# Fixed tile rotation two units deep, quartered low parts of w_down's sums, and a last layernorm with one GpSimd pass

## The chip, the cores and the metric

The kernel runs on one core of one Trainium2 chip. The metric is the device time of one execution in microseconds (us), the median over several runs. Five engines work side by side, each in its own order: TensorE (PE, matrix products into the PSUM banks; PEld is its weight load), VectorE (DVE), ScalarE (ACT), GpSimd (POOL) and SyncE (SP), which issues all DMAs here.

## What is computed

One decoder layer in float32 for 1024 tokens of width 1024: a token mixer (one input projection, a spatial gating half and a causal convolution half, one output projection) with a residual layernorm, then a gated MLP with a second one. The MLP and the last layernorm are what most of the change touches:

```
h    = causal_depthwise_conv(x1 @ w_up, conv_f_w, conv_f_b)      # 1024 x 5632, conv width 3
gate, val = h[:, :2816], h[:, 2816:]
ffn  = (silu(gate) * val) @ w_down                               # 2816 x 1024
out  = layernorm(1.189 * x1 + ffn, ln2_g, ln2_b)                 # rows of 1024
```

## The kernel before

Every float32 operand of a matrix product is split in two: a high part, rounded to the type that TensorE multiplies (a CAST on ACT), and a low part, what is left over (a subtraction on POOL or DVE). A product is three matmuls: high by high, high by low, low by high. The helper `split` does it for all of them, so the casts stand at L75 and the subtractions at L78.

**Input and output projections.** Sixteen column blocks of w_in are loaded through the pool `raw` (6 tiles of 128x1024), several ahead of use, then eight row blocks of w_out through the same pool (`load_wo`). `ln1` writes x1; `x1_T` and `x1_T2` transpose it.

**Up projection.** w_up's columns are cut into NF = 22 units: unit f is 128 gate and 128 value columns by all 1024 tokens. Unit 0 is a plain product (`first_steps`, 96 matmuls of 128x512: 2 column groups, 2 token halves, 8 row blocks, 3 matmuls each); its own matmuls alternate with the transposes of the second half of x1 (`x1_T2`), and `x1_sums` makes four sums of x1's quarters, t1 to t4, and splits them. From unit 1 on a unit is one step of Winograd's form of Strassen's product (`unit`): 7 products of 12 matmuls, 84 instead of 96. They take x1's quarters (b11, b21, b22 and t1 to t4) and the unit's weights and four sums of them. `prep_unit(f)` makes these: sums s1, s2 (tile `sa`) and s3, s4 (tile `sb`) on DVE, and seven splits (`wa`, `wb`, four `ws`, `wd`). When a unit's products are in PSUM, `conv3` applies the width-3 convolution: one ACT pass and two DVE passes of 128x1023 for the gate (`cg`), then as many for the value (`cv`), a SiLU, the product of the two, and a store to `hd[f]` in DRAM. Gate and value sums take two PSUM tiles a unit, and there are tiles for two units: a unit's first product writes where the unit before the last one was, so it waits until that one's `cg` passes have read it.

**Down projection.** It is of the same form: w_down's blocks are taken in NP = 11 pairs of units (kp), and each needs sums of w_down's quarters. Those are made during the up projection, at times that the table `sum_at` sets (a unit for each kp): `sum_load` reads two blocks of 512 KB (`dq`), `sum_prep` makes four sums on DVE (L813 to L816), two casts of 128x1024 on ACT (`dsh`) and two subtractions of 128x1024 on POOL, and stores the four results of 512 KB to DRAM. In the down loop `down_prep` is called ahead of a block: `wop_prep` reads them back (`ds`), loads and splits the plain parts (`db` to `dh`, `dl`), `hop_prep` does as much for the activations (`hr` to `ho`, sums `hs`). PE's products of this phase are at L930, and DVE adds each result to the row tiles x1r (L941, L946). At the end `finish` normalizes two row blocks, p and p+4, of a token pair, and `finish_last` those of the last pair.

**What sets the order.** Each engine executes in its own order, fixed when the program is built by a scheduler. It places the instructions by a simulated timeline: program order, `tc.high_priority` and `tc.issue_after` move them. Tiles come from pools of a few buffers each; a tile that is asked for waits until the last reader of the oldest one is done, so which buffer is reused, and when, comes out of the schedule.

## Time and profile before

| | us |
|---|---|
| median of 3 runs (lowest to highest) | 1046.07 (1046.02 to 1049.15) |
| the profiled execution | 1044.81 |
| its span in the trace | 1043.0 |
| PE busy in the span | 961.4 (92%) |
| DVE busy | 787.2 (75%) |
| POOL busy | 622.3 (60%) |
| ACT busy | 460.7 (44%) |

The times of the trace count from the start of the span; 1.8 us of the profiled execution lie outside it. The mean clock that TensorE was granted over the span is 0.963 of full. The stretches are: input and output projections to 301 us, up projection from 301.13 to 780.6 us (unit 0 to 336.16), down projection from 782 to 1017 us, the last row blocks to 1043 us. Of the chain that ended last, PE holds 57% and DVE 23%. A row of the timeline view gives start, duration, engine, line, operation, output and inputs, shape, and in brackets how long the engine had been idle and what ended that. Matmuls overlap: the pitch is read from their starts.

### The profile page before, as it was taken

How to read it: one execution, taken by the hardware profiler on the slowest of the kernel's cores; microseconds unless marked ns; L12 is line 12 of the kernel's file. 1: busy time of each engine (PE TensorE's matmuls, PEld its weight loads, DVE VectorE, ACT ScalarE, POOL GpSimd, SP SyncE). 2: the span in 40 equal slices, each digit the busy share in tenths (PEclk: the TensorE clock that was granted, in tenths of full speed). 3: DMA queues.
4: the chain of work that ended last, by engine and by line, in shares of the span. 5: the costliest groups of instructions: out<-in, count | busy, mean ns of one | idle time of the engine just before them, and what ended most of it. 6: DMA issues, size and time to landing. Idle time of an engine off the chain costs nothing.

```text
span 1043.0 us, 11987 instructions
## 1 busy us (share of the span) xinstructions
PE 961.4 (92%) x4200; PEld 781.5 (75%) x4200; DVE 787.2 (75%) x1062; ACT 460.7 (44%) x673; POOL 622.3 (60%) x391
## 2 busy tenths in 40 slices
...
GB/s 350 80 41 62 61 81 61 57 26 75 188 52 30 122 101 236 187 142 122 236 167 142 101 202 174 186 104 162 170 325 341 199 195 195 214 177 185 47 28 134
DMA packets 51627, 150.11 MB, mean 144 GB/s; under 512 B 5104, under 2 KB 16752, under 8 KB 51568
## 3 DMA queue, kind: packets, MB, share of 16 engines
...
q14 instruction: 26, 0.21, 0.1%
...
## 4 chain that ended last, share of the span: by engine, by line
PE 57%; DVE 23%; POOL 6%; issue 5%; DMA 5%; ACT 3%; SPq 0%; POOLq 0%; DVEq 0%; ACTq 0%
PE ps L215 15%; PE xy L930 12%; PE upv L624 10%; PE po L537 8%; PE upg L624 8%; DVE cg L636 3%; POOL dq L78 3%; DMA hr<-hd 3%; PE z L930 2%; DVE sa L693 2%; POOL ws L78 2%; DVE sa L694 2%; DVE cv L636 2%; DVE sb L699 1%; DMA ur<-in_w_up 1%
## 5 line engine op out<-in xcount | busy, mean ns | idle before, releaser
L930 PE MATMUL xy<-ds,ho 128*128 128x512 f32 x528 | 132.5, 399 | 11.1 <-DVE x1r L946 6.2
L263 DVE SCALAR_TENSOR_TENSOR acc<-ybin,cv,acc 128x512 f32<-128x512 f32 x196 | 134.3, 744 | 0.9 <-ACT acc L257 0.3
L946 DVE TENSOR_TENSOR x1r<-xy,x1r 128x512 f32<-128x512 f32 x117 | 80.3, 690 | 65.3 <-PE xy L930 64.9
L930 PEld LDWEIGHTS xy<-ds,ho 128*128 128x128 f32 x528 | 99.7, 191 | 38.1 <-DVE x1r L946 10.0
L78 POOL TENSOR_TENSOR ws<-sb,ws 128x512 fp32r<-128x512 f32 x42 | 58.0, 1380 | 62.9 <-ACT ws L75 62.9
L78 POOL TENSOR_TENSOR ho<-hr,ho 128x1024 fp32r<-128x1024 f32 (+1 forms) x24 | 55.6, 2315 | 50.3 <-ACT ho L75 50.3
L78 POOL TENSOR_TENSOR ws<-sa,ws 128x512 fp32r<-128x512 f32 x42 | 60.2, 1435 | 33.2 <-ACT ws L75 26.8
L624 PE MATMUL upv<-b11h,wa 128*128 128x512 f32 x168 | 57.0, 400 | 21.3 <-DVE cg L636 21.2
L930 PE MATMUL xy<-dh,ho 128*128 128x512 f32 x220 | 64.3, 396 | 6.2 <-POOL dh L78 3.7
L78 POOL TENSOR_TENSOR dq<-dq,dsh 128x1024 fp32r<-128x1024 f32 x22 | 57.3, 2619 | 10.0 <-ACT dsh L75 7.8
L624 PE MATMUL upv<-t2h,ws 128*128 128x512 f32 x168 | 57.4, 403 | 6.0 <-ACT pa L713 5.9
L624 PE MATMUL upg<-t1h,ws 128*128 128x512 f32 x168 | 61.7, 430 | 0.4 <-DVE upg L715 0.4
L636 DVE SCALAR_TENSOR_TENSOR cg<-upg,cv,cg 128x1023 f32<-128x1023 f32 (+4 forms) x46 | 56.6, 1230 | 6.1 <-ACT cg L633 5.2
L624 PE MATMUL upg<-b21h,wb 128*128 128x512 f32 x168 | 58.0, 390 | 0.0
L75 ACT CAST ho<-hr 128x1024 fp32r<-128x1024 f32 (+1 forms) x24 | 23.5, 978 | 77.2 <-issue 48.8
L636 DVE SCALAR_TENSOR_TENSOR cv<-upv,cv,cv 128x1023 f32<-128x1023 f32 (+4 forms) x46 | 56.6, 1230 | 1.2 <-ACT cv L633 0.5
L78 POOL TENSOR_TENSOR wa<-ur,wa 128x512 fp32r<-128x512 f32 x21 | 29.0, 1381 | 46.2 <-ACT wa L75 46.2
L624 PEld LDWEIGHTS upv<-b11h,wa 128*128 128x128 f32 x168 | 32.1, 191 | 32.2 <-issue 25.3
L693 DVE TENSOR_TENSOR sa<-ur 128x512 f32<-128x512 f32 x21 | 32.8, 1560 | 30.6 <-POOL ws L78 22.9
L624 PE MATMUL upv<-t3h,ws 128*128 128x512 f32 x168 | 55.1, 389 | 0.0
L624 PE MATMUL upv<-t4h,wd 128*128 128x512 f32 x168 | 55.1, 389 | 0.0
L624 PE MATMUL upg<-b22h,ws 128*128 128x512 f32 x168 | 55.1, 389 | 0.0
...
## 6 DMA issues: line engine op xcount, KB each, us to landing
ur<-in_w_up SPq DMA_DIRECT2D x44, 512.0 KB, 3.5
hd<-cg SPq DMA_DIRECT2D x22, 512.0 KB, 4.2
dq<-in_w_down SPq DMA_DIRECT2D x22, 512.0 KB, 6.0
dsh<-dsh SPq DMA_DIRECT2D x22, 512.0 KB, 2.7
dsl<-dq SPq DMA_DIRECT2D x22, 512.0 KB, 2.7
ds<-dsh SPq DMA_DIRECT2D x22, 512.0 KB, 4.4
ds<-dsl SPq DMA_DIRECT2D x22, 512.0 KB, 5.2
...
```

The costliest lines, as they stand in the source:

```text
L75: nc.scalar.copy(hi, raw)
L78: lo_eng.tensor_tensor(out=lo, in0=raw, in1=hi.bitcast(F32), op=ALU.subtract)
L215: nc.tensor.matmul(ps[hf] if isinstance(ps, list) else ps[:, ts(hf, 512)], wt[:, ts(k, P)], xt(k, hf), start=first and k == 0, stop=(not f ...
L263: nc.vector.scalar_tensor_tensor(out=xs(0) if k == 0 else acc, in0=xs(k), scalar=w(k), in1=first if n == 0 else acc, op0=ALU.mult, op1=ALU ...
L537: nc.tensor.matmul(po[:, ts(hf, 512)], a, b[:, ts(hf, 512)], start=first and i == 0, stop=last and i == 2)
L624: nc.tensor.matmul(out, w[a][:, ts(k, P)], x[b][k // 2][:, k % 2], start=first and k == 0 and i == 0, stop=last and k == 3 and i == 2, ski ...
L636: nc.vector.scalar_tensor_tensor(out=c[:, o:b], in0=ps[:, o - sh : b - sh], scalar=w(k), in1=c[:, o:b], op0=ALU.mult, op1=ALU.add,)
L693: tt(out=s1, in0=a21, in1=a22, op=ALU.add)
L694: tt(out=s2, in0=s1, in1=a11, op=ALU.subtract)
L699: tt(out=s4, in0=a12, in1=s2, op=ALU.subtract)
L930: nc.tensor.matmul(bank, hops[n][q][a][:, i, ts(j, P)], wops[kp][q][b], start=first and i == 0 and c == 0, stop=last and i == len(ks) - 1 ...
L946: nc.vector.tensor_tensor(out=dst if out is None else out, in0=bank, in1=dst, op=ALU.add)
```

## The change

It has six parts.

1. **Staging tiles.** The pool `raw` of 6 becomes two groups of 3 in the same memory, `raw` and `raw2`; loads of w_in and w_out have only the first.
2. **Start of the up projection.** `x1_sums` makes t1 and t2 only; `x1_sums2` makes t3, t4 and all splits after the last of those. Unit 0's second token half is computed in quarters of 256 columns, so that the first of them needs only two of the four transposed row blocks. Unit 1 becomes a plain product as well (96 matmuls instead of 84).
3. **Fixed rotation.** `keep` makes a tile once and returns it again: w_up's blocks, sa, sb, pa in two copies each (unit f uses copy f mod 2), operand tiles `wop` in eight, down weights `W` in three sets, `ho` and `hr` in two.
4. **Sums of w_down.** The table `sum_at` takes kp in every second unit, and the sums are cut in quarters of 128x512 (`sum_part`), called between the splits of `prep_unit`: a cast, a subtraction and two stores of 256 KB each. For kp = 0 they are made last, stay in SBUF (`dz`) and are split in `wop_prep`: nothing is stored or read back for it.
5. **Down operands.** The order of the loads at the end of the up projection is other, and `hop_load(1)` follows the loads of x1.
6. **Last layernorm.** In `finish` the row block p is treated like p+4: one DVE pass, an ACT pass and one POOL addition, the last two in halves, in place of an ACT pass and two POOL passes.

```diff
-    ) as ap_, tc.tile_pool(name="b", bufs=16) as bp, tc.tile_pool(name="raw", bufs=6) as rawp, tc.tile_pool(
+    ) as ap_, tc.tile_pool(name="b", bufs=16) as bp, tc.tile_pool(name="raw", bufs=3) as rawp, tc.tile_pool(
...
+
+        def raw2(name, shape=(P, 1024), dt=F32):
+            return rawp.tile(list(shape), dt, tag="raw2", name=name, bufs=3)
...
+        kept = {}
+
+        def keep(name, make):
+            if name not in kept:
+                kept[name] = make()
+            return kept[name]
...
-                    t = xt(f"ur{f}_{i}")
+                    t = keep(("ur", f % 2, i), lambda: xt(f"ur{f % 2}_{i}"))
...
         def op_tile(name, n):
-            if n % 2:
-                t = wp.tile([P, 1024], F32R, tag=("whi", "wlo")[n // 2 % 2], name=name, bufs=2)
...
-                t = A(F32R, name)
+            def make():
+                if n % 2:
+                    return wp.tile([P, 1024], F32R, tag=("whi", "wlo")[n // 2 % 2], name=f"wop{n % 8}", bufs=2)
+                return A(F32R, f"wop{n % 8}")
+
+            t = keep(("o", n % 8), make)
             return t[:, 0:512], t[:, 512:1024]
...
-        nop = [0]
+        nop = [1]
...
-            sa, sb = xt(f"sa{f}"), xt(f"sb{f}")
+            sa, sb = (keep((q, f % 2), lambda: xt(f"{q}{f % 2}")) for q in ("sa", "sb"))
...
+            part(0)
             tt(out=s3, in0=a11, in1=a21, op=ALU.subtract)
             w[7] = split_op(s3, f"ws3{f}")
+            part(1)
             tt(out=s4, in0=a12, in1=s2, op=ALU.subtract)
             w[3] = split_op(s4, f"ws4{f}")
+            part(2)
             w[4] = split_op(a22, f"wd{f}")
+            part(3)
...
+        def first_steps(f, q, hf, ks, part=None):
+            a0, a1 = (0, 512) if part is None else (part * 256, part * 256 + 256)
+            for k in ks:
+                for n, (a, b) in enumerate(((0, 0), (0, 1), (1, 0))):
+                    nc.tensor.matmul(
+                        ups[f][q][:, hf * 512 + a0 : hf * 512 + a1], whole[f][q][a][:, ts(k, P)],
+                        xb[k // 4, hf][b][k % 4 // 2][:, k % 2, a0:a1], start=k == 0 and n == 0,
+                        stop=k == KT - 1 and n == 2,
+                    )
...
                 sl = ts(s % 4, P)
-                ta, tb = (xt(f"tq{s}_{i}").rearrange("p (a c d) -> p a c d", a=2, c=4) for i in range(2))
-                t1, t2, t3, t4 = ta[:, 0], ta[:, 1], tb[:, 0], tb[:, 1]
+                t = xt(f"ta{s}").rearrange("p (a c d) -> p a c d", a=2, c=4)
+                tsum[s] = t[:, 0], t[:, 1]
+                t1, t2 = tsum[s]
...
-                    q = slice(2 * i, 2 * i + 2)
...
+                for i, q in enumerate(half):
+                    tt(out=t1[:, q], in0=tps[0][:, q], in1=braw[i][:, :, sl], op=ALU.subtract)
                     tt(out=t2[:, q], in0=tps[1][:, q], in1=t1[:, q], op=ALU.subtract)
-                    tt(out=t3[:, q], in0=t2[:, q], in1=raw, op=ALU.subtract)
-                    tt(out=t4[:, q], in0=xb[1, 0][0][i][:, :, sl].bitcast(F32), in1=t2[:, q], op=ALU.subtract)
-                    tt(out=t4[:, q], in0=t4[:, q], in1=xb[1, 0][1][i][:, :, sl].bitcast(F32), op=ALU.add)
+                last_sum[0] = nc.cur_bb.bb.instructions[-1]
...
+            def x1_sums2(s):
+                sl = ts(s % 4, P)
+                t1, t2 = tsum[s]
+                t = xt(f"tb{s}").rearrange("p (a c d) -> p a c d", a=2, c=4)
+                t3, t4 = t[:, 0], t[:, 1]
+                tt = nc.vector.tensor_tensor
+                with tc.issue_after(last_sum[0]):
+                    for i, q in enumerate(half):
+                        tt(out=t3[:, q], in0=t2[:, q], in1=braw[i][:, :, sl], op=ALU.subtract)
+                        tt(out=t4[:, q], in0=xb[1, 0][0][i][:, :, sl].bitcast(F32), in1=t2[:, q], op=ALU.subtract)
+                        tt(out=t4[:, q], in0=t4[:, q], in1=xb[1, 0][1][i][:, :, sl].bitcast(F32), op=ALU.add)
...
-            for q in range(2):
-                first_steps(q, 1, range(KT))
-            prep_unit(1)
+            for c in range(2):
+                for q in range(2):
+                    first_steps(0, q, 1, range(KT), c)
+            for t in range(4, 8):
+                x1_sums2(t)
+            with tc.high_priority(offset=PRIO):
+                whole[1] = [wsplit(load(w_up[1 + i * NF], f"ur1_{i}"), f"u1_{i}") for i in range(2)]
...
-        sum_at = {2 + kp * 17 // 10: kp for kp in range(NP)}
+        sum_at = {2 * kp - 1: kp for kp in range(1, NP)}
+        sum_at[NF - 1] = 0
...
-        def sum_prep(kp):
+                draw[kp] = []
+                for i in range(2):
+                    t = keep(f"dq{i}", lambda: raw2(f"dq{i}")) if kp else raw2(f"dz{i}")
...
-            wsum[kp] = []
-            for i, w in enumerate((w0, w1)):
-                hi = rawp.tile([P, 1024], F32R, tag="raw", name=f"dsh{i}_{kp}")
-                lo = w.bitcast(F32R)
-                split(w, hi, lo, nc.scalar, nc.gpsimd)
-                for q, t in (("h", hi), ("l", lo)):
-                    d = dp.tile([P, 1024], F32, name=f"ds{q}{i}_{kp}")
-                    nc.sync.dma_start(d, t.bitcast(F32))
...
+        def sum_part(kp, i):
+
+            w = draw[kp][i // 2][:, ts(i % 2, 512)]
+            hi = keep("dsh", lambda: raw2("dsh", dt=F32R))[:, ts(i % 2, 512)]
+            lo = w.bitcast(F32R)
+            nc.scalar.copy(hi, w)
+            with tc.issue_after(last_pool[0]):
+                nc.gpsimd.tensor_tensor(out=lo, in0=w, in1=hi.bitcast(F32), op=ALU.subtract)
+            if i == 0:
+                wsum[kp] = [[dp.tile([P, 1024], F32, name=f"ds{q}{j}_{kp}") for q in "hl"] for j in range(2)]
+            for d, t in zip(wsum[kp][i // 2], (hi, lo)):
+                nc.sync.dma_start(d[:, ts(i % 2, 512)], t.bitcast(F32))
...
+            b0 = rp.tile([P, 512], F32, tag="R", name=f"db0_{kp}")
...
+            ops = [wtile(kp, i) for i in range(4)]
+            if kp:
+                for i, d in enumerate(wsum[kp][0] + wsum[kp][1]):
+                    nc.sync.dma_start(ops[i].bitcast(F32), d)
...
+        def wop_prep(kp):
+            if kp not in wops:
+                wop_load(kp)
+            b0, b1, ops = wops[kp]
+            h0, h1, l1 = (wtile(kp, i) for i in (4, 5, 6))
+            split(b0, h0[:, 0:512], h0[:, 512:1024], nc.scalar, nc.gpsimd)
+            if not kp:
+                for i in range(2):
+                    split(draw[0][i], ops[2 * i], ops[2 * i + 1], nc.scalar, nc.gpsimd)
...
-                unit(f)
+                if f == 1:
+                    for hf in range(2):
+                        first_steps(1, 0, hf, range(KT))
+                    for hf in (1, 0):
+                        first_steps(1, 1, hf, range(KT))
+                else:
+                    load_unit(f + 1)
+                    unit(f)
                 if f in sum_at:
                     sum_load(sum_at[f])
+                kp = sum_at.get(f - 1)
+                if kp:
+                    sum_add(kp)
+                    prep_unit(f + 1, lambda i: sum_part(kp, i))
+                else:
+                    prep_unit(f + 1)
...
-                    hop_load(1)
-                prep_unit(f + 1)
-                if f - 1 in sum_at:
-                    sum_prep(sum_at[f - 1])
-                if f == NF - 1:
+                    sum_add(0)
                     down_prep(0)
                     for t in (2, 6, 3, 7, 0, 4, 1, 5):
                         load_x1(t)
+                    hop_load(1)
                     down_prep(1)
...
-                v.tensor_tensor(out=t, in0=mn, in1=y, op=ALU.mult)
-                affine(p, y[:, 0:1], t[:, 0:1])
-                xt4 = xr_[p + 4]
-                v.scalar_tensor_tensor(out=xt4, in0=xt4, scalar=mn[:, 1:2], in1=g2, op0=ALU.add, op1=ALU.mult)
-                nc.scalar.activation(xt4, xt4, AF.Copy, scale=y[:, 1:2])
-                nc.gpsimd.tensor_tensor(out=xt4, in0=xt4, in1=b2, op=ALU.add)
-                nc.sync.dma_start(out[p + 4], xt4)
+                for i in range(2):
+                    q = xr_[p + 4 * i]
+                    v.scalar_tensor_tensor(out=q, in0=q, scalar=mn[:, i : i + 1], in1=g2, op0=ALU.add, op1=ALU.mult)
+                    for a, b in ((0, 512), (512, 1024)):
+                        nc.scalar.activation(q[:, a:b], q[:, a:b], AF.Copy, scale=y[:, i : i + 1])
+                        nc.gpsimd.tensor_tensor(out=q[:, a:b], in0=q[:, a:b], in1=b2[:, a:b], op=ALU.add)
+                    nc.sync.dma_start(out[p + 4 * i], q)
```

How the order moves is shown at three places; rows are those of the engine's program order, and numbers in names tell tiles apart.

VectorE, up projection, a unit whose prepared weights stand beside w_down's sums (unit 9's results are in upg_4159 and cg_4302). Before:

```order
L722 TENSOR_TENSOR upg_4159<-upg_4159,pa_4165 128x512
L693 TENSOR_TENSOR sa_4553<-ur_1_4459 128x512
L694 TENSOR_TENSOR sa_4553<-sa_4553,ur_0_4457 128x512
L636 SCALAR_TENSOR_TENSOR cg_4302<-upg_4159,cv,cg_4302 128x1023
L697 TENSOR_TENSOR sb_4554<-ur_0_4457,ur_1_4459 128x512
L699 TENSOR_TENSOR sb_4554<-ur_0_4457,sa_4553 128x512
L636 SCALAR_TENSOR_TENSOR cg_4302<-upg_4159,cv,cg_4302 128x1022
L715 TENSOR_TENSOR upg_4314<-upg_4314,pa_4320 128x512
L636 SCALAR_TENSOR_TENSOR cv_4307<-upv_4160,cv,cv_4307 128x1023
```

After, a unit of the same kind (unit 10, upg_4250, cg_4386):

```order
L735 TENSOR_TENSOR upv_4251<-upv_4251,pb 128x512
L736 TENSOR_TENSOR upg_4250<-upg_4250,pa_3151 128x512
L637 SCALAR_TENSOR_TENSOR cg_4386<-upg_4250,cv,cg_4386 128x1023
L637 SCALAR_TENSOR_TENSOR cg_4386<-upg_4250,cv,cg_4386 128x1022
L729 TENSOR_TENSOR upg_4398<-upg_4398,pa_3305 128x512
L703 TENSOR_TENSOR sa_3247<-ur_1_3149 128x512
L708 TENSOR_TENSOR sb_3248<-ur_0_3147,ur_1_3149 128x512
L637 SCALAR_TENSOR_TENSOR cv_4391<-upv_4251,cv,cv_4391 128x1023
```

Before, sums for a later unit stand ahead of and between the two `cg` passes; now both passes follow the last addition at once, and the sums come behind them. Next unit's addition (L715 before, L729 now) follows the `cg` passes in both.

In the unit after that one (unit 11, no sums of w_down) the order after is another:

```order
L651 TENSOR_TENSOR cg_4386<-cg_4386,cv_4391 128x1024
L735 TENSOR_TENSOR upv_4399<-upv_4399,pb 128x512
L736 TENSOR_TENSOR upg_4398<-upg_4398,pa_3305 128x512
L637 SCALAR_TENSOR_TENSOR cg_4512<-upg_4398,cv,cg_4512 128x1023
L637 SCALAR_TENSOR_TENSOR cg_4512<-upg_4398,cv,cg_4512 128x1022
L703 TENSOR_TENSOR sa_3106<-ur_1_2640 128x512
L708 TENSOR_TENSOR sb_3107<-ur_0_2638,ur_1_2640 128x512
L729 TENSOR_TENSOR upg_4524<-upg_4524,pa_3151 128x512
L704 TENSOR_TENSOR sa_3106<-sa_3106,ur_0_2638 128x512
L637 SCALAR_TENSOR_TENSOR cv_4517<-upv_4399,cv,cv_4517 128x1023
```

Here two sums for a unit two ahead (L703, L708) stand between the `cg` passes and the next unit's addition L729.

GpSimd, the splits of a unit with w_down's sums. Before:

```order
L78 TENSOR_TENSOR ws_4267<-sa_4257,ws_4267 128x512
L78 TENSOR_TENSOR ws_4270<-sa_4257,ws_4270 128x512
L78 TENSOR_TENSOR ws_4274<-sb_4258,ws_4274 128x512
L78 TENSOR_TENSOR dq_4_4098<-dq_4_4098,dsh_4_4288 128x1024
L78 TENSOR_TENSOR dq_4_4100<-dq_4_4100,dsh_4_4295 128x1024
L78 TENSOR_TENSOR ws_4278<-sb_4258,ws_4278 128x512
L78 TENSOR_TENSOR wb_4421<-ur_0_4316,wb_4421 128x512
```

After (wop are the operand tiles, L860 the quarters):

```order
L81 TENSOR_TENSOR wop_3130<-sa_3247,wop_3130 128x512
L81 TENSOR_TENSOR wop_3249<-sb_3248,wop_3249 128x512
L81 TENSOR_TENSOR wop_3119<-ur_0_2638,wop_3119 128x512
L860 TENSOR_TENSOR dq_3102<-dq_3102,dsh 128x512 x2
L81 TENSOR_TENSOR wop_3108<-sb_3248,wop_3108 128x512
L860 TENSOR_TENSOR dq_3104<-dq_3104,dsh 128x512
L81 TENSOR_TENSOR wop_3111<-ur_1_3149,wop_3111 128x512
L860 TENSOR_TENSOR dq_3104<-dq_3104,dsh 128x512
L81 TENSOR_TENSOR wop_3123<-sa_3106,wop_3123 128x512
```

Two subtractions of 128x1024 in a row became four of 128x512, the last two between the unit's own.

GpSimd at units 0 and 1, after (u_0l, u_1l: unit 1's plain weights; t1l to t4l: x1's sums); before, the splits of unit 1's Strassen operands (wa and those after it) stood among the same t's:

```order
L81 TENSOR_TENSOR t3l_2630<-tb_2901,t3h_2628 128x2x128
L81 TENSOR_TENSOR t3l_2631<-tb_2901,t3h_2629 128x2x128
L81 TENSOR_TENSOR u_0l<-ur_0_2970,u_0h 128x1024
L81 TENSOR_TENSOR t4l_2634<-tb_2878,t4h_2632 128x2x128
L81 TENSOR_TENSOR t3l_2630<-tb_2924,t3h_2628 128x2x128
L81 TENSOR_TENSOR t3l_2631<-tb_2924,t3h_2629 128x2x128
L81 TENSOR_TENSOR t4l_2635<-tb_2878,t4h_2633 128x2x128
L81 TENSOR_TENSOR t4l_2634<-tb_2901,t4h_2632 128x2x128
L81 TENSOR_TENSOR t4l_2635<-tb_2901,t4h_2633 128x2x128
L81 TENSOR_TENSOR u_1l<-ur_1_2976,u_1h 128x1024
L81 TENSOR_TENSOR t3l_2630<-tb_2947,t3h_2628 128x2x128
L81 TENSOR_TENSOR t3l_2631<-tb_2947,t3h_2629 128x2x128
```

The low part of unit 1's weights stands after 20 of the 32 splits of t1 to t4, and twelve more follow it.

## Rows read from the trace of the kernel before

**Rows 1.** By stretch: length, busy us (instructions) per engine, clock, DMA share, GB/s.

```profile
325.00:350.00 25.00, 20.49 (x75) 16.10 (x74) 24.93 (x31) 13.23 (x28) 24.08 (x23) 0.84 0.25 85
525.00:550.00 25.00, 21.72 (x89) 17.32 (x87) 16.38 (x14) 9.00 (x14) 13.48 (x11) 0.93 0.39 136
```

**Rows 2.** The chain that ended last: start, us, what, instructions.

```profile
763.61 2.72 PE upv L624 x12
```

**Rows 3.** Waits of TensorE, 400 to 780 us: total us, times, longest.

```profile
PE upv L624 <- DVE cg L636: 21.2, 8, 3.4
```

**Rows 4.** TensorE's timeline: first matmuls of units 0, 6, 11, 20; others.

```profile
301.13 0.39 PE L773 MATMUL upg<-b11h,u0h 128*128 128x512 f32 x1
...
429.83 0.47 PE L624 MATMUL upv<-b11h,wa 128*128 128x512 f32 x1 [0.21 <-DVE cg L636]
...
535.94 0.47 PE L624 MATMUL upv<-b11h,wa 128*128 128x512 f32 x1 [3.28 <-DVE cg L636]
...
536.48 0.64 PE L624 MATMUL upg<-t1h,ws 128*128 128x512 f32 x1
...
540.91 0.62 PE L624 MATMUL upv<-b11h,wa 128*128 128x512 f32 x2
...
729.65 0.47 PE L624 MATMUL upv<-b11h,wa 128*128 128x512 f32 x1 [3.28 <-DVE cg L636]
...
780.22 0.39 PE L624 MATMUL upv<-t4h,wd 128*128 128x512 f32 x1
```

**Rows 5.** Timeline of VectorE ahead of unit 11's first product.

```profile
527.02 1.76 DVE L693 TENSOR_TENSOR sa<-ur 128x512 f32<-128x512 f32 x1 [1.79 <-POOL ws L78]
...
531.61 1.33 DVE L697 TENSOR_TENSOR sb<-ur,ur 128x512 f32<-128x512 f32 x1
...
534.53 1.27 DVE L636 SCALAR_TENSOR_TENSOR cg<-upg,cv,cg 128x1022 f32<-128x1022 f32 x1
```

**Rows 6.** Timeline of GpSimd there: w_down's low parts, then the unit's own.

```profile
503.88 2.84 POOL L78 TENSOR_TENSOR dq<-dq,dsh 128x1024 fp32r<-128x1024 f32 x1
...
520.51 5.22 POOL L78 TENSOR_TENSOR dq<-dq,dsh 128x1024 fp32r<-128x1024 f32 x2 [0.68 <-ACT dsh L75]
525.70 1.29 POOL L78 TENSOR_TENSOR ws<-sb,ws 128x512 fp32r<-128x512 f32 x1
```

**Rows 7.** Timeline of TensorE, units 0 and 1: one transpose row, two waits.

```profile
302.27 1.03 PE L739 MATMUL x1u<-ident,xres 128*128 128x128 f32 x8
...
323.16 0.80 PE L773 MATMUL upg<-b12l,u0h 128*128 128x512 f32 x1 [3.20 <-DVE b12l L78]
...
346.45 0.79 PE L624 MATMUL upv<-t2h,ws 128*128 128x512 f32 x1 [4.51 <-ACT pa L713]
```

**Rows 8.** Group by line and shape, 300 to 350 us: busy us, mean ns.

```profile
L78 POOL TENSOR_TENSOR t2l<-tq,t2h 128x256 fp32r<-128x256 f32 x8 | 7.9, 1003 | 15.1 <-ACT t2h L75 15.1
```

**Rows 9.** DMA issues of the page: count, KB each, median us to landing.

```profile
ur<-in_w_up SPq DMA_DIRECT2D x44, 512.0 KB, 3.5
...
dsh<-dsh SPq DMA_DIRECT2D x22, 512.0 KB, 2.7
```

**Rows 10.** Timeline of the transition to the down projection, GpSimd and TensorE.

```profile
779.35 1.30 POOL L78 TENSOR_TENSOR ho<-hr,ho 128x512 fp32r<-128x512 f32 x1 [14.32 <-ACT ho L75]
...
786.59 2.08 PE L930 MATMUL xy<-dh,ho 128*128 128x512 f32 x4 [3.68 <-POOL dh L78]
```

**Rows 11.** Timeline of the last rows, VectorE, then GpSimd.

```profile
1005.14 1.28 DVE L1015 SCALAR_TENSOR_TENSOR x1r<-x1r,fin,g2row 128x1024 f32<-128x1024 f32 x1
...
1015.74 2.30 DVE L106 SCALAR_TENSOR_TENSOR rowl<-rowl 128x1 f32<-128x1 f32 x1
...
1025.99 2.36 DVE L1015 SCALAR_TENSOR_TENSOR x1r<-x1r,fin,g2row 128x1024 f32<-128x1024 f32 x1
...
1015.65 2.37 POOL L987 TENSOR_TENSOR x1r<-x1r,g2row 128x1024 f32<-128x1024 f32 x1
...
1034.76 2.34 POOL L987 TENSOR_TENSOR x1r<-x1r,g2row 128x1024 f32<-128x1024 f32 x1
```

132 lines of the change are left out of this document (68 added, 64 removed).

## The prediction

> **What bounds the kernel now.** I read first the page's shares (PE 92% busy, mean granted clock 0.963), then the table by stretches of 25 us for the places where PE is not full, then PE's waits there, then the timelines of the engines that are waited for. PE is the bound by the sum; what can be won is the time in which it stands or runs slowly. Twelve matmuls take 2.72 us at full speed [rows 2], a pitch of 0.2267 us, so a Strassen unit of 84 matmuls needs 19.04 us and a plain one of 96 needs 21.76 us. The up projection runs from 301.13 to 780.22 + 0.39 = 780.61 us, 479.5 us in all [rows 4]. From the first matmul of unit 6 (429.83) to that of unit 20 (729.65) fourteen units take 299.8 us, against 14 x 19.04 = 266.6: 33.2 us are lost, 2.4 us a unit [rows 4]. The table of waits gives 21.2 us of it in 8 waits, all of one kind: the first product of a unit waits for the DVE pass `cg` that frees its PSUM bank [rows 3].
>
> The reader should see what stands ahead of that pass. Ahead of unit 11, POOL spends 5.22 us at one go on the low parts of w_down's sums (520.51), so the unit's own low part comes at 525.70 [rows 6]. The DVE sum `sa` waits for POOL (idle 1.79 us, start 527.02), and since DVE works in order, the two `sa`, the two `sb` and only then the second `cg` follow, from 534.53 [rows 5]. PE stands 3.28 us. After that its clock is low: the twelve matmuls from 536.48 to 540.91 take 4.43 us, 1.71 more than at full speed [rows 4], and the stretch has a granted clock of 0.93 [rows 1], part of it on the lower of the two levels (1.2 GHz against 2.4). Such a stall costs about 5.0 us. In 325 to 350 us another engine is the bound: DVE 24.93 and POOL 24.08 us busy of 25 [rows 1], since x1's sums, their splits and unit 1's preparation all fall there; PE waits 3.20 and 4.51 us [rows 7].
>
> **The change part by part.** The sum is made against the profiled execution, 1044.81 us.
>
> *Steady loop.* Per unit PE's work is unchanged, so its ideal is 20 x 19.04 = 380.8 us for units 2 to 21. By the new order both `cg` passes stand right behind the last addition (L736), and the prepared sums behind them. From the unit's last gate product that path is 0.7 (addition), 1.2 (ACT pass) and 2 x 1.27 us [rows 5], 4.5 to 5 us; PE has 34 further matmuls, 7.7 us, to do before it needs the bank. Slack 2.6 us, so I cost these stalls at nothing; the cover is those 34 matmuls, and without it the price is the old 5.0 us. The low parts in quarters are 4 x 1.3 us on POOL [1.29 for this shape, rows 6] in place of 5.22, so none of POOL's work goes away; it only no longer stands in one piece. Their copies on ACT stand ahead of the `cg` pass: I reckon the last one 13.0 to 13.6 us into the unit and `cg` at 14.9, a slack of 1.4 us, with two waits for stores at 2.7 us each [rows 9]. SP issues eight stores a pair of units instead of four; nothing on PE's path is queued behind them but w_up's loads, which have a unit's time.
>
> A new wait remains in every second unit, the one without sums of w_down: there L703 and L708, for a unit two ahead, stand before the addition L729 that PE needs for its t1 product. L703 waits for w_up's next block, whose tile, now one of two, is free only once POOL has split the old one. I put that issue at 16.2 us into the unit, landing 3.5 us later [rows 9], at 19.7; two sums of 0.7 to 1.76 us [rows 5] and L729 itself (0.7) end at 21.8 to 23.9 us. PE needs it at 19.04 + 2.72 + 2 matmuls = 22.2. The stall is between 0 and 1.7 us; I take 1.0, being nearer the sums' contended length, and at 10 such units 10 us (0 to 17). One that short need not lower the clock.
>
> *Start.* Unit 0: 21.76 us, 32 transposes at 1.03 us for 8 [rows 7], 4.1 us, and 96 matmuls of 256 columns in place of 48 of 512. Exactly half the pitch would add nothing; halfway between the 128-column row (0.129) and 0.2267 gives 0.162 and 96 x 0.162 - 10.88 = 4.7 us. I take 1 (ends 0 and 4.7), since the row's 1.03 holds the run-out of the last matmul. Unit 1 as a plain product costs 12 x 0.2267 = 2.7 us more. In return it needs none of t1 to t4: POOL's 32 low parts at about 1.0 us [rows 8] lie beside units 0 and 1, 47 us of PE time. But unit 1's weights stand on POOL after 20 of them, and their tiles come free only when PE has done with unit 0's: a wait of 1 to 2 us, then one for the second half; 3 us with some clock (0 to 6). Together 26.9 + 21.8 + 3 = 51.7 us.
>
> Up projection: 51.7 + 380.8 + 10 = 442.5 us against 479.5, so **-37.0 us**.
>
> *Staging tiles.* w_out loads run three ahead instead of six, and I reckon the last low part some 4 us later; PE takes eight row blocks in turn, so most of it is covered. +1 us (0 to 3).
>
> *Transition.* For kp = 0 four stores and four loads of 512 KB go away, but two POOL passes of 128x1024 (2.3 to 2.8 each, the single ones in [rows 6, 11]), two casts and four DVE sums come in just there. POOL is idle for 14.32 us before 779.35, and PE waits 3.68 us for POOL's `dh` after it [rows 10]. The two passes fit into that idle time if their loads land in unit 21; if not they stand ahead of `ho` and cost 5 to 6 us. I take -2 us (-8 to +6).
>
> *Last layernorm.* Three `finish` calls lose a POOL pass of 2.3 to 2.4 us each and gain a DVE pass of 1.28 alone or 2.36 beside POOL [rows 11]. At the very end two row blocks wait in a row on POOL: three passes before, two after, and halves let ACT and POOL overlap. Also, a DVE step of one column takes 2.30 us while a POOL pass runs (1015.74 beside 1015.65) [rows 11], and fewer passes hold it up less. I take -4 us, between 0 and -7.
>
> The trace thus shows a DVE step held for about as long as a POOL pass runs. The Trainium skill (SBUF — State Buffer, section "SBUF: two separate sides") calls the port pair of the two an exclusive lock, which whoever comes first holds for its whole instruction. That speaks against this edit: the new DVE passes, with two inputs in SBUF, would hold POOL out in turn, three times 1.2 us of the 4, and the term would be near -0.4.
>
> Sum: 1044.81 - 37.0 + 1 - 2 - 4 = 1002.8 us. The median lies 1.26 us above the profiled execution, so **1004 us**.
>
> **Rivals.**
>
> *The change doesn't take the stalls out.* If DVE or ACT runs later than I reckon by 2 to 3 us, every second unit keeps a full stall of 5.0 us with its low clock: 10 x 5.0 instead of 10, so +40, 1044 us. For it speaks that DVE's sums take up to 1.76 us beside POOL, and L703 waits for a transfer. Against: in each unit DVE and POOL have idle time left, 8.6 and 11.5 us of 25 in [rows 1]. If only half of these units do so, it is +20, 1024 us.
>
> *Slower.* The two copies that wait for a store hold ACT in order, and with it the `cg` pass. Slack is 1.4 + 2.6 = 4.0 us; with a landing of L us it is exceeded by 2 x (L - 2.7) - 4.0. At L = 7 that is 4.6 us, with 1.7 for the clock 6.3 us in ten units, 63 in place of 10: 1057 us. It turns the result slower than before from L = 6.6 on. Against: 2.7 us for twice the size [rows 9], though stores now come in pairs beside w_up's loads.
>
> The Trainium skill (DMA: Bandwidth & Descriptors, section "Anatomy of one DMA — SWDGE (gpsimd) path") gives a DMA a fixed part of about 2.0 us besides its bytes at 436 GB/s; from it I estimate 2.6 us for 256 KB, so halving a store saves little, and a 512 KB one 3.2, where the row has 2.7. Had the landing halved with the size, I would give this rival 0.03.
>
> *No stall at all.* Were w_up's load issued some 2 us earlier, the 10 us vanish: 994 us.
>
> **How the numbers follow.** The forecast with its terms' ends (990 to 1020) gets 0.63; stalls left in half of the second units (1024) 0.13; in all of them (1044) 0.07; slower (1057) 0.07; no stall (994, in the forecast's range) 0.10. About 0.3%, 3 us, is what a measurement of this kernel can tell from no change. Faster by more: 0.63 + 0.13 + 0.10 = 0.86; the case at 1044 is mostly within it: 0.06; slower: 0.08. A range to 1032 takes in the forecast, the stall-free case and the half case, and leaves out 0.14 and some of the tails.
>
> **What would show it.** Right: full stretches of 25 us from 360 us on with a granted clock of 1.00 and no wait for `cg`; waits of at most 1.7 us for L729 in every second unit; the first matmul of the down projection near 743 us; unit 1 without DVE at 24.9 of 25. Wrong: waits of PE over 3 us in the loop, with clocks of 0.93; ACT idle for a store ahead of `cg`; the end of the trace more than 30 us behind the last matmul; POOL's W splits ahead of `ho` with PE waiting.

## The result and the profile after

The changed kernel takes **1018.25 us** in the median (1013.88 to 1023.76, 4 runs) against 1046.05 us for the kernel before (1044.94 to 1049.15): a ratio of 0.9732, with a 95% interval of 0.9681 to 0.9784. The forecast was 1004 us, within 990 to 1032. The profiled execution of after took 1018.08 us, with a span of 1016.3 us. Its span is 26.7 us shorter than that of before, and the difference divides so:

| stage (us) | before | after | measured | forecast |
|---|---|---|---|---|
| start to unit 0's first matmul | 301.13 | 299.41 | -1.7 | +1 |
| up projection (22 units) | 479.3 | 453.3 | -26.0 | -37.0 |
| down projection | 236.6 | 242.8 | +6.2 | -2 |
| last matmul to the end | 26.0 | 20.8 | -5.2 | -4 |

Here, and for every kernel below, the up projection goes from the first matmul of unit 0 to the end of its last product, the down projection from there to the end of the last matmul. Stages are good to about 0.2 us, since the end of a matmul is modelled in the trace.

The page of after, part 1 and the clock row of part 2 (the granted clock in tenths, 40 slices):

```profile
span 1016.3 us, 12231 instructions
...
PE 952.0 (94%) x4260; PEld 774.0 (76%) x4260; DVE 762.3 (75%) x1055; ACT 460.9 (45%) x691; POOL 613.4 (60%) x409
...
PEclk9999999999999999999999999999998999999996
```

PE's waits in after, by what ended them (us in all, how many, the longest):

```profile
PE xy L1015 <- DVE x1r L1031: 15.0, 15, 1.9
PE xy L1015 <- DVE x1r L1026: 6.5, 5, 2.4
PE upg L625 <- DVE upg L729: 4.2, 4, 1.2
PE upv L625 <- DVE upv L735: 2.5, 1, 2.5
PE upv L625 <- DVE cg L637: 2.3, 1, 2.3
...
PE upg L743 <- POOL u_0l L81: 2.0, 1, 2.0
```

The waits for `cg` have gone from 8 with 21.2 us [rows 3] to one of 2.3 us. What grew is the group at the top, waits of the down projection for an addition. In the loop proper, 400 to 725 us, PE ran 1410 matmuls at a granted clock of 1.00, where before ran 1298 at 0.97; 112 more at 0.2267 us [rows 2] are 25.4 us. The table by stretches, of before and then of after (columns as in [rows 1]):

```profile
400.00:725.00 325.00, 305.06 (x1298) 247.74 (x1297) 245.81 (x220) 156.95 (x221) 199.18 (x128) 0.97 0.45 164
```

```profile
400.00:725.00 325.00, 321.46 (x1410) 263.74 (x1409) 235.10 (x235) 167.55 (x252) 206.02 (x150) 1.00 0.47 167
```

DVE's timeline in one unit of after (start, duration, engine, line, tiles, then the idle time ahead and what ended it) answers to [rows 5]:

```profile
554.18 0.70 DVE L736 TENSOR_TENSOR upg<-upg,pa 128x512 f32<-128x512 f32 x1 [1.79 <-PE upg L625]
556.15 2.60 DVE L637 SCALAR_TENSOR_TENSOR cg<-upg,cv,cg 128x1023 f32<-128x1023 f32 x2 [1.27 <-ACT cg L634]
559.12 0.69 DVE L703 TENSOR_TENSOR sa<-ur 128x512 f32<-128x512 f32 x1 [0.37 <-DMA ur<-in_w_up]
559.73 1.79 DVE L708 TENSOR_TENSOR sb<-ur,ur 128x512 f32<-128x512 f32 x1
561.44 0.69 DVE L729 TENSOR_TENSOR upg<-upg,pa 128x512 f32<-128x512 f32 x1
```

Both `cg` passes now follow the last addition directly, and the prepared sums come behind them. They still come early: the product that needs them starts at 597.22 us, 38 us later.

### The profile page after: what moved, and what is told of

Same layout as the page of the kernel before. It is cut to its first block, busy times and chain, and to the rows that moved or that the text cites. A ratio compares the mean times of both kernels' runs of the same rounds, so it can differ in the third digit from the quotient of the medians.

```text
span 1016.3 us, 12231 instructions
## 1 busy us (share of the span) xinstructions
PE 952.0 (94%) x4260; PEld 774.0 (76%) x4260; DVE 762.3 (75%) x1055; ACT 460.9 (45%) x691; POOL 613.4 (60%) x409
## 4 chain that ended last, share of the span: by engine, by line
PE 63%; DVE 20%; issue 4%; DMA 4%; POOL 4%; ACT 3%; SPq 1%; POOLq 0%; DVEq 0%; ACTq 0%
PE upv L625 18%; PE upg L625 15%; PE xy L1015 11%; PE ps L218 8%; PE po L540 8%; DVE acc L266 6%; PE z L1015 2%; DVE hr L949 2%; DVE x1r L1031 2%; POOL wop L81 2%; POOL ho L81 1%; DMA hr<-hd 1%; DMA ur<-in_w_up 1%; DVE hs L948 1%; DVE hs L951 1%
## 5 line engine op out<-in xcount | busy, mean ns | idle before, releaser
L1015 PE MATMUL xy<-W,ho 128*128 128x512 f32 x792 | 193.9, 398 | 21.9 <-DVE x1r L1031 15.0
L1015 PEld LDWEIGHTS xy<-W,ho 128*128 128x128 f32 x792 | 148.3, 190 | 63.6 <-DVE x1r L1031 23.4
L1031 DVE TENSOR_TENSOR x1r<-xy,x1r 128x512 f32<-128x512 f32 x117 | 79.8, 689 | 63.4 <-PE xy L1015 63.3
L81 POOL TENSOR_TENSOR wop<-ur,wop 128x512 fp32r<-128x512 f32 x60 | 83.4, 1391 | 57.8 <-ACT wop L78 57.8
L81 POOL TENSOR_TENSOR wop<-sb,wop 128x512 fp32r<-128x512 f32 x40 | 54.9, 1374 | 48.9 <-ACT wop L78 48.9
L81 POOL TENSOR_TENSOR wop<-sa,wop 128x512 fp32r<-128x512 f32 x40 | 58.7, 1466 | 33.3 <-issue 30.4
L625 PE MATMUL upg<-t1h,wop 128*128 128x512 f32 x160 | 53.7, 396 | 4.2 <-DVE upg L729 4.2
L860 POOL TENSOR_TENSOR dq<-dq,dsh 128x512 fp32r<-128x512 f32 x40 | 55.9, 1407 | 0.7 <-ACT pa L727 0.7
L625 PE MATMUL upv<-t4h,wop 128*128 128x512 f32 x160 | 53.8, 397 | 2.5 <-DVE upv L735 2.5
L625 PE MATMUL upg<-b22h,wop 128*128 128x512 f32 x160 | 52.8, 391 | 2.2 <-ACT pb L733 2.2
L625 PE MATMUL upv<-t3h,wop 128*128 128x512 f32 x160 | 52.8, 391 | 0.8 <-ACT pa L731 0.8
```

The costliest lines, as they stand in the source:

```text
L81: lo_eng.tensor_tensor(out=lo, in0=raw, in1=hi.bitcast(F32), op=ALU.subtract)
L625: nc.tensor.matmul(out, w[a][:, ts(k, P)], x[b][k // 2][:, k % 2], start=first and k == 0 and i == 0, stop=last and k == 3 and i == 2, ski ...
L860: nc.gpsimd.tensor_tensor(out=lo, in0=w, in1=hi.bitcast(F32), op=ALU.subtract)
L1015: nc.tensor.matmul(bank, hops[n][q][a][:, i, ts(j, P)], wops[kp][q][b], start=first and i == 0 and c == 0, stop=last and i == len(ks) - 1 ...
L1031: nc.vector.tensor_tensor(out=dst if out is None else out, in0=bank, in1=dst, op=ALU.add)
```

## The experiments

Every kernel's stages from its profiled execution, with the medians of its runs and the ratio to the kernel before, run on the same chip in turn. Not all rows come from one chip, so rows are compared by their ratios:

| kernel | up | down | end | median us | ratio (95%) |
|---|---|---|---|---|---|
| before | 479.3 | 236.6 | 26.0 | 1046.05 | 1 |
| after | 453.3 | 242.8 | 20.8 | 1018.25 | 0.9732 (0.9681 to 0.9784) |
| e7: before, quarters alone | 473.8 | 239.2 | 26.2 | 1040.79 | 0.9942 (0.9915 to 0.9968) |
| e2: after, four quarters at one point | 457.0 | 247.6 | 20.6 | 1023.92 | 0.9806 (0.9771 to 0.984) |
| e9: before, sums late | 531.7 | 241.1 | 26.0 | 1103.15 | 1.0554 (1.0524 to 1.0583) |
| e10: before, sums and cg exchanged | 448.0 | 234.5 | 26.1 | 1011.99 | 0.968 (0.9646 to 0.9713) |
| e1: after, old last layernorm | 457.1 | 243.2 | 26.3 | 1023.86 | 0.9807 (0.976 to 0.9853) |
| e4: after, hop sums held | 450.0 | 247.0 | 20.6 | 1020.17 | 0.9759 (0.9733 to 0.9785) |
| e6: after, kp = 0 early | 452.6 | 244.1 | 20.8 | 1018.86 | 0.9746 (0.9715 to 0.9777) |
| e13: after, unit 3's sums held | 450.8 | 244.9 | 20.9 | 1019.81 | 0.9758 (0.9719 to 0.9797) |
| e3: after, L949 on GpSimd | 453.1 | 238.8 | 20.2 | 1016.48 | 0.9727 (0.9691 to 0.9764) |
| e8: e3 and e4 | 449.8 | 244.4 | 20.2 | 1017.03 | 0.9726 (0.9694 to 0.9758) |
| e11: after, two sums on GpSimd | 454.0 | 232.9 | 20.2 | 1008.96 | 0.9654 (0.9624 to 0.9684) |
| e14: e11 and e13 | 450.7 | 235.0 | 20.2 | 1005.71 | 0.9615 (0.9585 to 0.9645) |

### Which part takes the stalls out: quarters or order?

**e7**, the kernel before with the low parts of w_down's sums in quarters between the unit's own, and no other part of the change. w_down's sums on DVE now come before the unit's preparation, and the order on DVE is not the old one: `sa` and `sb` stand ahead of both `cg` passes, not ahead of and between them.

```
-                prep_unit(f + 1)
                 if f - 1 in sum_at:
-                    sum_prep(sum_at[f - 1])
+                    kp = sum_at[f - 1]
+                    sum_prep(kp)
+                    prep_unit(f + 1, lambda i: sum_part(kp, i))
+                else:
+                    prep_unit(f + 1)
...
```

> The kernel before with one part of the change alone: w_down's sums in quarters between the unit's own splits, at the units where they stood, tiles as before. On VectorE the sums sa and sb of a later unit now stand ahead of both cg passes instead of between them. Theory A (the pieces on GpSimd made the stalls): the eight waits for cg, 21.2 us, shrink to less than a third, and the time falls to 1015 to 1030 us. Theory B (the place of cg behind sa and sb on VectorE made them): the waits stay at 15 us or more, and the time stays at 1040 to 1050 us.

Its largest wait in the loop:

```profile
PE upg L624 <- DVE upg L719: 15.8, 8, 3.9
```

The up projection is 5.5 us shorter. Eight waits stay, now for an addition instead of `cg` (one more of 3.6 us is still for `cg`). In DVE's order the sums still stand ahead of the `cg` passes, and the addition behind them.

**e2**, the other way round: after, with the four quarters called at one point of the unit, behind the fifth of its seven splits. In the trace GpSimd then does them two and two (3.00 and 2.56 us) with one split between.

```
-                    prep_unit(f + 1, lambda i: sum_part(kp, i))
+                    prep_unit(f + 1, lambda i: [sum_part(kp, j) for j in range(4)] if i == 1 else None)
```

> The changed kernel with the four quarters of w_down's sums asked for at one point of the preparation (behind the fourth split), so that GpSimd does them two and two with one split between. The order of the cg passes on VectorE is as in the changed kernel, right behind the last addition. Theory A: the up projection lost its stalls because the low parts no longer stand in one piece; then waits of TensorE for cg of about 3 us come back in units with sums, the clock falls to 0.93 to 0.95 in their stretches, and the time is 1040 to 1065 us. Theory B: it lost them because cg follows the addition at once; then no such wait comes back, and the time stays within 1013 to 1024 us.

The long stalls don't come back: one wait of 2.3 us for `cg`, as in after, and 7 waits for L729 with 7.7 us. The up projection is 3.7 us longer, the down projection 4.8 us (one wait of 6.15 us at 762.81 us, not followed further). The 3.7 us can't be given to the quarters, since e1 (below) has the same 7 waits with after's own loop.

**e9** and **e10** take the rest of the change away and leave only the order: the kernel before, with the prepared sums held behind a `cg` pass. In e9 the sums of unit f + 1 wait for the second pass of unit f (s3 and s4 as s1 and s2; `gate_tile`, which makes the passes, is called ahead of `prep_unit` for it):

```
+            return tc.issue_after(last_cg[0]) if last_cg[0] else tc.high_priority(offset=0)
...
+            with hold():
+                tt(out=s1, in0=a21, in1=a22, op=ALU.add)
+                tt(out=s2, in0=s1, in1=a11, op=ALU.subtract)
...
+                cg = gate_tile(f)
                 prep_unit(f + 1)
...
```

> The kernel before with one change: the DVE sums that prepare the next unit (L693 to L699) are held behind the second cg pass of the unit that PE has just done. Tiles, loads, the low parts of w_down's sums in one piece, kp = 0 and the last layernorm are as before. Theory (DVE's order is what removes the stalls): the 8 waits of 21.2 us for cg go with their slow matmuls; the up projection takes 455 to 462 us in place of 479.3, and the time is 1022 to 1032 us. Rival (the order is only possible at no cost with loads two units ahead and the quarters): the prepared sums then come late, PE waits as long for the prepared operands or for the addition L715, as the kernel with the quarters alone did (15.8 us in 8 waits), and the time is 1037 to 1047 us.

Neither side foresaw what came: 57 us slower than before. Its waits, and the first sum of one unit:

```profile
PE upg L624 <- ACT ws L75: 42.0, 16, 4.2
```

```profile
441.44 0.68 DVE L700 TENSOR_TENSOR sa<-ur 128x512 f32<-128x512 f32 x1
```

This is unit 5's first sum. The unit's t2 product, which needs the sum made from it, starts at 445.61 us, 4.2 us later; in before the same distance is 49.8 us for unit 13 (547.75 to 597.59). I had read the sums as those of the next unit, and they were those of a unit further on. Held for the next unit's, they lost the lead in which ACT and GpSimd split them. e10 mends that: the sums of unit f wait for the second `cg` pass of unit f - 3, and `gate_tile` is where it was.

```
+            return tc.issue_after(cgs[f - 3]) if f - 3 in cgs else tc.high_priority(offset=0)
...
+            with hold(f):
+                tt(out=s1, in0=a21, in1=a22, op=ALU.add)
+                tt(out=s2, in0=s1, in1=a11, op=ALU.subtract)
...
```

> The kernel before with one change: the DVE sums of unit f are held behind the second cg pass of unit f - 3, so that they keep the lead they had (about two units) and only change places with the cg pass that they stood in front of. Tiles, loads, w_down's low parts in one piece, kp = 0 and the last layernorm are as before. Theory (that order is what removes the stalls): the 8 waits of 21.2 us for cg and their slow matmuls go, and few others come; the up projection takes 457 to 463 us in place of 479.3, the time is 1024 to 1031 us. Rival (the stall is passed on, as in the kernel with the quarters alone, where 8 waits of 15.8 us for an addition came in place of those for cg): up projection 470 us or more, time 1037 to 1047 us. Second rival (sums that start later make the operands late, as in the kernel that held them for unit f - 1): slower than before.

```profile
PE upv L624 <- ACT pa L722: 4.9, 2, 4.4
...
PE upg L624 <- DVE upg L724: 3.2, 4, 1.2
...
PE upv L624 <- DVE cg L636: 0.8, 1, 0.8
```

```profile
516.14 2.51 POOL L78 TENSOR_TENSOR dq<-dq,dsh 128x1024 fp32r<-128x1024 f32 x1 [2.48 <-ACT dsh L75]
...
518.62 1.28 POOL L78 TENSOR_TENSOR ws<-sb,ws 128x512 fp32r<-128x512 f32 x1
...
519.87 2.39 POOL L78 TENSOR_TENSOR dq<-dq,dsh 128x1024 fp32r<-128x1024 f32 x1
...
520.20 2.60 DVE L636 SCALAR_TENSOR_TENSOR cg<-upg,cv,cg 128x1023 f32<-128x1023 f32 x2 [1.45 <-ACT cg L633]
...
522.71 1.35 DVE L700 TENSOR_TENSOR sa<-ur 128x512 f32<-128x512 f32 x1
```

GpSimd's whole passes of 2.4 to 2.5 us are still there, `cg` waits for nothing but ACT, and the sums keep a lead of about 40 us (522.71 to 562.73 for unit 12). That edit alone gives 1012.0 us, 34.5 us below before on the same chip: at least as much as the whole change, whose interval of the ratio overlaps with this one's. From 400 to 725 us it runs 1412 matmuls, after 1410. So the exchange on DVE is enough for the loop's whole gain, after has this order too, and the quarters aren't needed for it. No run gave after the old order, and which part of the new staging made the scheduler exchange them was not tried. The up projection is 448.0 us, 5.3 less than after's. Most of that is the end of unit 21: its last 60 matmuls, from its t2 product on, take 13.6 us in before and in e10, as they should at full pitch, and 20.1 us in after.

### The start and the end of the up projection

After loses 8.3 us from the start of unit 2 to the t2 product of unit 4 (351.31 to 403.14 us, 192 matmuls in 51.8 us instead of 43.5); 6.1 us of them are waits. There the four sums of unit 3 still stand ahead of unit 1's `cg` passes, of which the last two are shown:

```profile
354.21 1.77 DVE L704 TENSOR_TENSOR sa<-sa,ur 128x512 f32<-128x512 f32 x1
356.01 1.66 DVE L711 TENSOR_TENSOR sb<-ur,sa 128x512 f32<-128x512 f32 x1
357.59 2.58 DVE L637 SCALAR_TENSOR_TENSOR cg<-upg,cv,cg 128x1023 f32<-128x1023 f32 x2
```

**e13** holds unit 3's sums behind unit 1's second `cg` pass (`issue_after(cgs[1])` if f is 3).

> The kernel after, with the DVE sums of unit 3 held behind unit 1's second cg pass. In the trace of after two of them (1.77 and 1.66 us) stand in front of that pass at 354 us, PE waits 2.28 us for it at 360.33, and units 2 and 3 together lose 6.1 us. Theory (this one place still has the order of before): the wait for cg goes, the ones behind it (1.18, 0.64, 1.58 us) shrink, up projection 449 to 451 us in place of 453.3, time 1014 to 1016 us. Rival (unit 1's late second half and ACT's queue set these waits): the wait changes its name, up projection 453 us, time 1018 us.

The pass starts at 351.80 us instead of 357.59 and the wait for `cg` is gone; a wait of 1.87 us for GpSimd's `wop` takes part of it. The up projection is 2.5 us shorter, as the theory had it, but the down projection 2.1 us longer, and the time is that of after within its interval.

In unit 21 the end of the queue is DVE's too (after):

```profile
740.28 1.19 DVE L849 TENSOR_TENSOR dz<-dz,dz 128x512 f32<-128x512 f32 x1 [1.91 <-DMA dz<-in_w_down]
...
745.48 0.85 DVE L948 TENSOR_TENSOR hs<-hr 128x256 f32<-128x256 f32 x1 [3.23 <-DMA hr<-hd]
...
747.52 0.69 DVE L735 TENSOR_TENSOR upv<-upv,pb 128x512 f32<-128x512 f32 x1
```

```profile
748.26 0.73 PE L625 MATMUL upv<-t4h,wop 128*128 128x512 f32 x1 [2.53 <-DVE upv L735]
```

L735, which PE needs, waits behind a sum whose load `hr` has not landed. PE then runs its last twelve matmuls from 748.26 to 752.72 us, 4.46 us instead of 2.72 [rows 2]. **e4** holds the four sums of `hop_prep` behind the unit's last addition, L736, so that L735 is ahead of them too:

```
+            last_add[0] = nc.cur_bb.bb.instructions[-1]
...
+            with tc.issue_after(last_add[0]):
+                tt(out=s1, in0=a21, in1=a22, op=ALU.add)
...
```

> The kernel after, with the four DVE sums of hop_prep for block 0 and block 1 held behind unit 21's last addition (L736). In the trace of after, unit 21's PE waits 2.53 us for L735, which stands in DVE's order behind sums that wait 3.23 us for the loads hr; the matmuls after that wait run at half clock. Theory (the head of DVE's queue is what the end of the up projection loses): the wait of 2.53 us falls below 0.7 us, its slow twelve matmuls (4.46 us in place of 2.72) become fast, and the up projection ends 3 to 4 us earlier, near 449 us in length in place of 453.3; the down projection keeps its length or loses 1 us, so about 1015 us. Rival (the transition is bound by block 0's operands whatever DVE's order): the same 3 to 4 us come back as longer waits of the first down products, and the time stays at 1018 us.

The up projection ends 3.3 us sooner, and then:

```profile
754.69 2.07 PE L1017 MATMUL xy<-W,ho 128*128 128x512 f32 x4 [4.33 <-ACT ho L78]
```

The down projection is 4.2 us longer, and the time is the rival's. Its mechanism is shown only in part, because ACT's order is another too. In after ACT casts block 0's `ho` ahead of a `W` whose load is late; in e4 it is the other way round, and `ho` waits with it (ACT, after, then e4):

```profile
747.91 0.61 ACT L78 CAST ho<-hr 128x512 fp32r<-128x512 f32 x1
...
752.66 1.05 ACT L78 CAST W<-db 128x1024 fp32r<-128x1024 f32 x1 [1.96 <-DMA db<-in_w_down]
```

```profile
753.07 1.04 ACT L78 CAST W<-db 128x1024 fp32r<-128x1024 f32 x1 [6.00 <-DMA db<-in_w_down]
754.02 0.61 ACT L78 CAST ho<-hr 128x512 fp32r<-128x512 f32 x1
```

Whether `ho` would have been late without this exchange on ACT was not tried. **e6** asks whether kp = 0's sums, kept in unit 21, are to blame; it forms them at unit 3 with stores and loads as for the others. (In it kp = 1's sums are formed from kp = 0's rows, since the one load overwrites the other's tiles; the work is the same, the output is not the layer's.)

```
-        sum_at[NF - 1] = 0
+        sum_at[2] = 0
...
```

> The kernel after, with kp = 0's sums formed at unit 3, stored and loaded again as the other pairs' are, so that the two GpSimd passes, two casts and four DVE sums of unit 21 are gone and four stores and four loads of 512 KB are back. Theory (these additions, in front of L735, and the passes ahead of ho make the end of the up projection late): the wait for dz (1.91 us) goes, unit 21 is 2 to 4 us shorter, and the down projection's early waits (1.1, 2.4 and 1.4 us) shrink; unit 4 pays about 1 us. 1013 to 1016 us. Rival, as the prediction had it (keeping them saves about 2 us, since loads of 2 MB then compete with hr): the end of unit 21 waits for hr instead, the down projection starts later, 1019 to 1022 us.

Up 452.6, down 244.1, time 1018.86 us: not the theory's gain, and a loss as small as the rival's lower end can't be told from the spread of after's runs. In the trace the cost has only changed its place: the last 60 matmuls of unit 21 lose 0.8 us instead of 6.5, and units 4 and 5, where the sums now fall, lose 6.3 us more than in after. In the sum, keeping kp = 0 costs and saves nothing that can be measured.

### The down projection

One block of after, GpSimd, DVE and PE (their timelines):

```profile
836.93 2.69 POOL L81 TENSOR_TENSOR ho<-hr,ho 128x1024 fp32r<-128x1024 f32 x1 [0.29 <-ACT ho L78]
837.38 0.69 DVE L1031 TENSOR_TENSOR x1r<-xy,x1r 128x512 f32<-128x512 f32 x1
837.99 2.18 DVE L949 TENSOR_TENSOR hr<-hr 128x512 f32<-128x512 f32 x1
...
840.10 0.68 DVE L950 TENSOR_TENSOR hs<-hs,hr 128x512 f32<-128x512 f32 x1
...
840.70 1.28 DVE L1031 TENSOR_TENSOR x1r<-xy,x1r 128x512 f32<-128x512 f32 x2
...
841.43 3.06 PE L1015 MATMUL xy<-W,ho 128*128 128x512 f32 x12 [1.36 <-DVE x1r L1031]
```

L949, both inputs and its output in SBUF, meets GpSimd's pass and ends only 0.55 us after it (839.62 and 840.17 us). The addition that frees PE's bank waits behind it. The same form alone takes 0.68 us. L1031, which reads PSUM, takes 0.69 us beside GpSimd. Over 790 to 990 us the same sum of 128x512 took, by groups (count, then busy time and mean ns), in before and in after:

```profile
L873 DVE TENSOR_TENSOR hr<-hr 128x512 f32<-128x512 f32 x9 | 9.4, 1041 | 0.1
```

```profile
L949 DVE TENSOR_TENSOR hr<-hr 128x512 f32<-128x512 f32 x8 | 13.1, 1632 | 0.0
```

It is so throughout the trace of after. From 301 to 995 us all 83 such sums that began during a GpSimd pass ended 0.54 to 0.67 us behind it, the 81 others took 0.68 to 0.69 us, and none of the 116 additions with an operand in PSUM that began during a pass took more than 0.70 us. In this order L949 meets such a pass in 7 of its 12 calls, in before L873 in 3 of 12.

The Trainium skill (SBUF — State Buffer, section "SBUF: two separate sides") describes an exclusive lock, held for the whole instruction, between a DVE instruction with two inputs in SBUF and a GpSimd one that reads SBUF; the trace agrees, as the end 0.55 us behind the pass shows.

**e3** moves this sum to GpSimd:

```
-            tt(out=a21, in0=a11, in1=a21, op=ALU.subtract)
+            nc.gpsimd.tensor_tensor(out=a21, in0=a11, in1=a21, op=ALU.subtract)
```

> The changed kernel with one of the four sums of the activations in the down loop (L949, which writes hr) done by GpSimd instead of VectorE. Theory: the down loop is 6 us longer than before because L949 takes 2.18 us where 0.69 would do, held up by a GpSimd pass over hr of 2.7 us, and the two additions to x1r behind it come late, which makes TensorE wait 1.36 to 1.49 us in six blocks; without it on VectorE these waits vanish, the down loop takes 234 to 236 us instead of 242.8, and the time is 1009 to 1012 us. Rival: GpSimd then has 1.3 us more in each block, its low parts for the next block come late, and TensorE waits for GpSimd instead: the down loop takes 242 us or more, the time is 1018 or above.

The down projection falls to 238.8 us, 4.0 of the 6.2 us; the time, 1016.48 us, can't be told from after's. From 777 to 877 us L950 is now the one that is held (1.4 to 2.8 us), and one long wait appears behind three sums in a row that are all held (1.57 to 2.72 us, from 784.48 us on):

```profile
791.33 9.22 PE L1015 MATMUL xy<-W,ho 128*128 128x512 f32 x30 [4.70 <-DVE x1r L1031]
...
837.61 3.01 PE L1015 MATMUL xy<-W,ho 128*128 128x512 f32 x12 [0.77 <-DVE x1r L1031]
```

**e8** joins e3 (from the second block on) and e4:

> Two edits in one: block 0's sums held as in the kernel with the held sums, and for all later blocks the in-place difference of hop_prep (L949) on GpSimd, which alone gave 1016.5 us with a down projection of 238.8 us in place of 242.8. Theory (the two losses are at different places and add up): up projection near 449 us, down projection near 239 us, 1011 to 1014 us. Rival (the wait of unit 21 only moves into the down projection): 1015 to 1017 us.

1017.03 us; the gains don't add, and the time is the rival's (4.5 us of waiting for `ho` at the first down product, with ACT's order as in e4). **e11** moves L949 and L950, but not in the first two blocks:

```
+            tg = nc.gpsimd.tensor_tensor if n > 1 else tt
-            tt(out=a21, in0=a11, in1=a21, op=ALU.subtract)
-            tt(out=s2, in0=s1, in1=a11, op=ALU.subtract)
+            tg(out=a21, in0=a11, in1=a21, op=ALU.subtract)
+            tg(out=s2, in0=s1, in1=a11, op=ALU.subtract)
```

> The kernel after, with the two sums L949 and L950 of hop_prep on GpSimd for all blocks but the first two. In the trace of after L949 takes 2.18 us in place of 0.69, since GpSimd holds it, and PE waits 1.36 us a block for an addition x1r behind it; with L949 alone on GpSimd the next sum, L950, was held for 2.18 us and PE waited 0.77 us a block, and one wait of 4.7 us came in the second block. Theory (DVE's passes from SBUF that meet a GpSimd pass are what lengthens the down projection): waits per block near 0.2 us, no wait of 4.7 us, a down projection of 235 to 237 us in place of 242.8, 1011 to 1013 us. Rival (GpSimd's longer chain delays ho): blocks as long as with the one pass, 20.1 us, down projection 239 to 241 us, 1015 to 1017 us.

```profile
834.14 1.30 POOL L950 TENSOR_TENSOR hr<-hr 128x512 f32<-128x512 f32 x1
...
835.40 1.30 POOL L951 TENSOR_TENSOR hs<-hs,hr 128x512 f32<-128x512 f32 x1
...
836.07 0.69 DVE L1032 TENSOR_TENSOR x1r<-xy,x1r 128x512 f32<-128x512 f32 x1 [0.67 <-PE xy L1016]
```

On GpSimd, each takes 1.30 us and DVE's additions come every 1.36 us. The down projection takes 232.9 us, below the 235 to 237 of the theory and below before's 236.6, and the time is 1008.96 us.

### The last layernorm, and the best kernel

**e1** is after with the old last layernorm (`affine` and `finish` of the kernel before).

> The changed kernel with the last layernorm of before in the three finish calls: row block p goes through one ACT pass and two GpSimd passes of 128x1024 again. TensorE's order is the same. Theory: the shorter end (20.8 us from the last matmul to the end of the span, against 26.0 before) comes from the GpSimd passes that fell away; then the end grows to 25 to 26 us and the time from 1018 to 1022 to 1024 us. Rival: the end is short because the order of the rows and of VectorE's steps is another; then it stays at 20 to 22 us and the time at 1018.

The end is 26.3 us long, 5.5 us more than in after and as in before, so the whole -5.2 us is this edit's. The run is 5.6 us slower in the median (8 us by the ratios), with a reservation: its up projection is 3.8 us longer too, though all engines' orders are those of after up to the tail. In it L729 makes PE wait 7 times, in after 4 times. The cause is a race. In every second unit L703 and L708 stand ahead of L729, and L703's load `ur` lands at about the time at which GpSimd starts a pass (after, GpSimd, DVE and PE, units 8 and 10):

```profile
481.34 1.82 POOL L81 TENSOR_TENSOR wop<-sa,wop 128x512 fp32r<-128x512 f32 x1 [3.33 <-issue]
...
481.31 0.69 DVE L703 TENSOR_TENSOR sa<-ur 128x512 f32<-128x512 f32 x1 [0.48 <-DMA ur<-in_w_up]
```

```profile
519.72 1.29 POOL L81 TENSOR_TENSOR wop<-sa,wop 128x512 fp32r<-128x512 f32 x1 [3.32 <-issue]
...
519.77 1.78 DVE L703 TENSOR_TENSOR sa<-ur 128x512 f32<-128x512 f32 x1 [0.56 <-DMA ur<-in_w_up]
...
523.93 0.50 PE L625 MATMUL upg<-t1h,wop 128*128 128x512 f32 x1 [1.17 <-DVE upg L729]
```

Whichever starts first holds up the other. In unit 8 DVE is 0.03 us ahead: L703 takes 0.69 us, the GpSimd pass 1.82 instead of 1.29, and PE doesn't wait. In unit 10 GpSimd is 0.05 us ahead: L703 takes 1.78 us and PE waits 1.17 us. The sixteen such meetings of units 4 to 18 in the two traces all go this way: DVE first in 7, without a wait worth counting; GpSimd first in 9, with a wait of 1.17 or 1.18 us. A unit that loses the race takes 20.5 us, one that wins it 19.2 to 19.4. After loses three, e1 six, and three times 1.2 us are nearly the whole 3.8 us. Differences of that size in one trace's up projection (e2, e6) prove nothing.

**e14**, e11 and e13 together, is the fastest kernel run here:

> The two edits together: unit 3's sums behind unit 1's cg, and two of the sums of hop_prep on GpSimd from the third block on. If both theories hold the gains add up, being 300 us apart: up projection 449 to 451 us, down projection 235 to 237 us, 1008 to 1010 us. If both rivals hold, 1015 to 1018 us.

1005.71 us (1003.34 to 1007.21), 0.9615 of before. Up 450.7 and down 235.0 are both within what the theory gave, and the time is below its 1008 to 1010 us; against e11 alone (1008.96 us) the gain is not clear of the two intervals. e10 with the new last layernorm, 5 us less by e1, was not run.

## Why the prediction was right, and where it was off

The sign and the chief mechanism were right: the stalls for `cg` were the loss, and DVE's order was what kept them. The forecast was 14 us too low (1004 against 1018), still within its range. By its steps:

- **Steady loop: right.** No stall for `cg` from unit 4 on, clock 1.00. From the t2 product of unit 4 to that of unit 20 (403.14 to 713.58 us) sixteen units took 310.4 us against 304.6 ideal: 5.8 us lost where I put 1.0 in every second unit, 8. The wait is 1.18 us and came in three of eight such units. That it was three is luck: hundredths of a us decide the race. And I gave the quarters a share of the cause; e10 shows that the exchange alone does it.
- **Start: mis-sized.** I had 3 us for unit 1's tiles. Unit 0 took 26.15 us (forecast 26.9) and unit 1 25.75, 4.0 over its 21.76 with its waits. The 8.3 us that units 2 and 3 lose I had put at nothing, as steady loop. (The pitch of 0.162 that I called halfway lies a third of the way between the two rows, by columns; halfway is 0.178. The trace has 0.12, near the end at which the pieces cost nothing.)
- **End of the up projection: missed.** 6.5 us in unit 21, where before loses nothing: three waits of 4.0 us, 1.7 us in the twelve slow matmuls, the rest in slower ones behind the shorter waits. I asked only whether GpSimd's passes would stand ahead of `ho`, not what DVE's queue would hold up. e6 takes nearly all of it away by moving kp = 0's sums, and pays as much in units 4 and 5; e4 takes 4.7 us of it away by order, and PE then waits for `ho`.
- **Transition, -2 us (-8 to +6), and the blocks behind it: the step that failed.** The down projection grew by 6.2 us, and not at the transition: its first 132 matmuls took 42.4 us, 5.3 less than in before (47.7). The other 792 took 200.4 us, 11.5 more (188.9). I gave the 14 blocks no term, because their work is unchanged; but in the new order a sum from SBUF meets a GpSimd pass in most of the calls, and PE's bank waits behind it. e11, which moves two such sums, takes 9.9 us off. What in the change brings them together was not tried.
- **Tail: right.** -5.2 us, forecast -4 (0 to -7). In after a one-column step takes 1.21 us (L109) where it took 2.30 [rows 11]; the new DVE pass L1091 takes 1.27 and 1.66 us. The lock's version, -0.4 us, did not come about here, though the lock itself shows in the down projection.
- **Stores.** The rival in which a store's landing holds ACT came only in small: ACT waited for one three times, 6.4 us in all and 2.7 at most, and no wait of PE for `cg` came of it. 256 KB land in 2.1 us (`dsh`) and 3.1 us (`dsl`); 2.7 us for twice the size [rows 9]. The Trainium skill's fixed part (DMA: Bandwidth & Descriptors, "Anatomy of one DMA — SWDGE (gpsimd) path") gave an estimate of 2.6 us, and the mean of the two agrees, though that section is on transfers that GpSimd issues and these are issued by SyncE; for 512 KB it gave 3.2.

The up projection took 453.3 us against a forecast of 442.5. These 10.8 us are the 8.3 of units 2 and 3 and the 6.5 of unit 21, less 4.2 in the loop. The down projection's 8.2 make up most of the rest, and the tail and the first stage give 3.9 back. Of that, 2.7 us are the first stage's, -1.7 against +1, which no run explains.
